# Fetching the first tokens ahead of the constants, on two queues, in chunks of 128

## The chip, the cores and the metric

The kernel runs on one core of one Trainium2 chip. The metric is the device time of one execution in microseconds (us); the times given are the median of three runs, and a profile is one further execution taken by the hardware profiler.

## What is computed

A decoder trunk of two layers over 1024 tokens, with 16 learned meta tokens put ahead of them (1040 rows of 1024 float32 values). Layer 0 mixes tokens with a gated DeltaNet, layer 1 with an mLSTM; each layer is then followed by a squared-ReLU MLP. Cut to what matters here, which is the very first step of layer 0:

```python
h = concatenate([meta, x], axis=1)              # (1, 1040, 1024)
y = h * rsqrt(mean(h * h, axis=-1) + 1e-6) * attn_norm[0]
proj = y @ gdn_in[0]                            # q, k, v, z, beta and a of 16 heads
qkv = silu(causal_conv(qkv, gdn_conv[0]))       # depthwise, 4 taps
# ... chunked delta rule, gated norm, output projection, residual, MLP; then layer 1
```

## The kernel before

Everything is float32, and large products are made in three passes: an operand is split into a high part in the rounded type float32r and a low part (what the rounding left), and `mm3` issues high times high, high times low and low times high (lines 116 to 118). Weights come in columns of 128: `load_split` fetches a column into a raw buffer (line 153), ACT casts the high part `whi` (line 156), and DVE subtracts for the low part `wlo` (line 157). There are two raw buffers and two pairs of split buffers.

The DeltaNet layer works on two halves of the tokens. The first half has 528 tokens (16 meta tokens and 512 of x), the second 512. For each half, `proj` runs through eight head pairs with several columns each. The first columns are K and Q of the first pair, and each takes all tokens of the half in two groups: `dense` makes eight times three products for a group, into the tile `ps_in`. Both groups of the first half have 264 tokens. The order at the very start is K group 0, Q group 0, K group 1, Q group 1, then the gate column (`gates_dense`, lines 138 and 139), then V.

Before any of that, the tokens must be normed, turned and split. `load_consts` builds masks on POOL and fetches the small norm and convolution vectors as rows (lines 208 to 212, on SP's queue); PE transposes them (line 215, tile `ps_nr`), and DVE copies them to `ncols` (line 217). Then `norm_in` takes the 528 tokens in five chunks: four of 112 and one of 80. For every chunk:

- SP's queue fetches the rows into a tile `nx` (lines 303 and 304);
- ACT squares them and sums (line 319), DVE scales the sum (line 320), POOL takes the power -1/2 (line 321), and DVE multiplies the rows by it (line 322);
- PE transposes the eight blocks of 128 columns into two PSUM tiles `pn` (line 329); the pool has two such tiles in all;
- for each of the two, DVE multiplies by the norm weights in `ncols` (line 331, tile `xw`), ACT casts the high part (line 334, tile `act_hi`) and DVE subtracts for the low part (line 335, tile `act_lo`).

The order of instructions on each engine is not the order of this text. A planner simulates the program with estimated times and writes each engine's instructions in the order that it finds; on the chip every engine then runs them strictly in that order, waiting on semaphores. Each DMA is issued by one engine's queue (here SP, and for a few transfers in the MLPs ACT).

Of the kernel before, what the change touches and what calls it, by code (L numbers as in the profile page):

```python
# [7 lines left out]
F32 = mybir.dt.float32  # L8
F32R = mybir.dt.float32r
AF = mybir.ActivationFunctionType  # L10
ALU = mybir.AluOpType
# [4 lines left out]
P = 128  # L16
D = 1024
KT = D // P
SEQ = 1024
META = 16  # L20
# [11 lines left out]
GS = 2 * GC  # L32
GL = (META + GC * P, GC * P)
GO = (META, 0)
XW = GL[0]
FF = 4096
HB = 4
# [18 lines left out]
class Ctx:  # L56
# [29 lines left out]
    def xact(self):  # L86

        return tuple(self.acts.tile([P, 2, XW], F32R, tag=t, name="act_" + t) for t in ("hi", "lo"))

# [93 lines left out]
def load_consts(c, attn_norm, ffn_norm, mlstm_norm, gdn_norm, gdn_conv):  # L183
    nc, k = c.nc, c.const
    c.ident = k.tile([P, P], F32, name="ident")
    make_identity(nc, c.ident)
    c.ones = k.tile([P, P], F32, name="ones")
    nc.gpsimd.memset(c.ones, 1.0)
    c.eps = k.tile([P, 1], F32, name="eps")
    nc.gpsimd.memset(c.eps, EPS)  # L190
    warm = k.tile([P, 1], F32, name="warm")
    nc.scalar.activation(warm, c.eps, AF.Square)
    c.rt = k.tile([NT, 2 * G // NT], F32, name="rt")
    c.half = k.tile([P, 1], F32, name="half")
    nc.gpsimd.memset(c.half, 0.5)
    c.mhalf = k.tile([P, 1], F32, name="mhalf")
    nc.gpsimd.memset(c.mhalf, -0.5)
    c.tri = k.tile([P, P], F32, name="tri")
    nc.gpsimd.memset(c.tri, 1.0)
    nc.gpsimd.affine_select(out=c.tri, in_=c.tri, pattern=[[1, P]], compare_op=ALU.is_ge, fill=0.0,  # L200
                            base=0, channel_multiplier=-1)
    c.mneg = k.tile([P, P], F32, name="mneg")
    nc.gpsimd.memset(c.mneg, 0.0)
    nc.gpsimd.affine_select(out=c.mneg, in_=c.mneg, pattern=[[1, P]], compare_op=ALU.is_ge, fill=NEG,
                            base=0, channel_multiplier=-1)
    rows = staging(c, [P, 2, P])
    nc.gpsimd.memset(rows[:, 1], 0.0)
    nc.sync.dma_start(out=rows[:, 0], in_=gdn_conv[0].rearrange("t (c p) -> (t c) p", p=P))
    nc.sync.dma_start(out=rows[0:16, 1], in_=attn_norm.rearrange("l (k p) -> (l k) p", p=P))
    nc.sync.dma_start(out=rows[16:32, 1], in_=ffn_norm.rearrange("l (k p) -> (l k) p", p=P))  # L210
    nc.sync.dma_start(out=rows[32:40, 1], in_=mlstm_norm.rearrange("l (k p) -> (l k) p", p=P))
    nc.sync.dma_start(out=rows[40:41, 1], in_=gdn_norm)
    ps = c.pj.tile([P, 2, P], F32, tag="pj", name="ps_nr")
    for j in range(2):
        nc.tensor.transpose(ps[:, j], rows[:, j], c.ident)
    cols = k.tile([P, 2, P], F32, name="ncols")
    nc.vector.tensor_copy(cols, ps)
    c.conv_w = cols[:, 0].rearrange("p (t c) -> p t c", t=4)
    c.attn_nw = [cols[:, 1, l * KT:(l + 1) * KT] for l in range(2)]
    c.ffn_nw = [cols[:, 1, 16 + l * KT:16 + (l + 1) * KT] for l in range(2)]  # L220
    c.mlstm_nw = cols[:, 1, 32:40]
    c.gdn_nnw = k.tile([P, 1], F32, name="gdn_nnw")
    nc.vector.tensor_scalar(c.gdn_nnw, cols[:, 1, 40:41], -1.0, None, op0=ALU.mult)


class GDN:
# [69 lines left out]
            nc.vector.tensor_copy(t, bc(self.idq, 1, GS))  # L296
            yield

    def x_rows(self, t0, n, xt=None):
        xt = (staging(self.c, [P, D]) if xt is None else xt)[:n]  # L300
        m = max(META - t0, 0)
        if m:
            self.nc.sync.dma_start(out=xt[0:m], in_=self.meta)
        self.nc.sync.dma_start(out=xt[m:n], in_=self.x[t0 + m - META:t0 + n - META])
        return xt

    def norm_in(self):

        nc, c, g2 = self.nc, self.c, self.g2
        self.xh = [c.xact() for _ in range(KT // 2)]  # L310
        tags = ("AB", "AB", "V", "V", "sz")
        rows = 112
        spans = [(t0, min(rows, GL[0] - t0)) for t0 in range(0, GL[0], rows)]
        junk = g2.tile([P, D], F32, tag="sz", name="njunk", bufs=3)
        xs = [self.x_rows(t0, n, g2.tile([P, D], F32, tag=tg, name="nx", bufs=3 if tg == "sz" else 2))
              for (t0, n), tg in zip(spans, tags)]
        for (t0, n), xt in zip(spans, xs):
            ss = self.p2.tile([P, 1], F32, tag="xs1", name="xs1", bufs=len(xs))[:n]
            nc.scalar.activation(junk[:n], xt, AF.Square, accum_out=ss)
            nc.vector.tensor_scalar(ss, ss, 1.0 / D, EPS, op0=ALU.mult, op1=ALU.add)  # L320
            nc.gpsimd.tensor_tensor(ss, ss, c.mhalf[:n], op=ALU.pow)
            nc.vector.tensor_scalar(xt, xt, ss[:, 0:1], None, op0=ALU.mult)
        for (t0, n), xn in zip(spans, xs):
            ts = slice(t0, t0 + n)
            for kk in range(2):
                ks = slice(kk * 4, kk * 4 + 4)
                pn = self.pp.tile([P, 4, P], F32, tag="pp", name="pn")[:, :, :n]
                for j in range(4):
                    nc.tensor.transpose(pn[:, j], xn[:, (kk * 4 + j) * P:(kk * 4 + j + 1) * P], c.ident[:n, :n])
                xw = self.p2.tile([P, 4, rows], F32, tag="raw", name="xw")[:, :, :n]  # L330
                nc.vector.tensor_tensor(xw, pn, bc(c.attn_nw[0][:, ks], 2, n), op=ALU.mult)
                for j in range(2):
                    hi, lo = (t[:, :, ts] for t in self.xh[2 * kk + j])
                    nc.scalar.copy(hi, xw[:, 2 * j:2 * j + 2])
                    nc.vector.tensor_tensor(lo, xw[:, 2 * j:2 * j + 2], hi.bitcast(F32), op=ALU.subtract)

    def h_init(self, cc):
# [3 lines left out]
        if cc >= HC:  # L341
            for kk in range(2):
                junk = self.p2.tile([P, XW], F32, tag="acc", name="xjunk")[:CH, :D // 2]
                nc.scalar.activation(junk, xt[:, kk * (D // 2):(kk + 1) * (D // 2)], AF.Square,
# [29 lines left out]
    def norm_pair(self, j):  # L374
# [4 lines left out]
        for i in range(2):  # L379
            k = 2 * j + i  # L380
            hk = self.p2.tile([P, 3 + XW], F32, tag="raw", name="hk")[:, :n]
            nc.sync.dma_start(out=hk, in_=self.dram["hT"][k, :, T - n:T])
# [6 lines left out]
    def gates_dense(self, hf):  # L389
# [6 lines left out]
        w = gates_split(c, wraw)  # L396
        self.ba = self.p1.tile([P, XW], F32, tag="ba", name="ba")
        for g in range(2):
# [4 lines left out]
    def tokens(self, hf, ci):  # L403

        t0 = GO[hf] + ci * P if ci < GC else 0
        return slice(t0, t0 + P)
# [56 lines left out]

    def dense(self, whl, hf, g):

        c, n = self.c, GL[hf] // 2
        ps = c.pj.tile([P, 512], F32, tag="pj", name="ps_in")[:, :n]
        gs = slice(g * n, (g + 1) * n)
        for k in range(KT):
            xhi, xlo = (x[:, k % 2, gs] for x in self.xh[k // 2])  # L470
            if isinstance(whl, tuple):
                mm3(self.nc, ps, whl[0][:, k], whl[1][:, k], xhi, xlo, k == 0, k == KT - 1)
            else:
                mm2(self.nc, ps, whl[:, k], xhi, xlo, k == 0, k == KT - 1)
            if k == KT // 2 - 1:
                yield
        return ps, gs

    def column(self, s, ct, out):
# [3 lines left out]
        n = GL[s["hf"]]  # L483
        raw = p2.tile([P, 3 + XW], F32, tag="raw", name="raw")
        nc.gpsimd.tensor_copy(raw[:, 0:3], self.hist[:, ct])
# [4 lines left out]
        if s["hf"] == 0:  # L490
            nc.gpsimd.tensor_copy(self.hist[:, ct], raw[:, n:n + 3])
        acc = p2.tile([P, XW], F32, tag="acc", name="acc")[:, :n]
        cw = c.conv_w[:, :, ct:ct + 1]
# [1192 lines left out]
def trunk(tc, x, meta_tokens, attn_norm, ffn_norm, ff_up, ff_down, gdn_in, gdn_conv, gdn_a_log, gdn_dt_bias,  # L1686
          gdn_norm, gdn_out, mlstm_in, mlstm_gate_bias, mlstm_norm, mlstm_out, out):
    nc = tc.nc
    with ExitStack() as st:
        c = Ctx(tc, st)  # L1690
        c.const = c.pool("const", 1)
        dp = c.pool("dram", 1, space=DRAM)
        dram = {
            "hT": dp.tile([KT, P, T], F32, name="d_hT"),
            "o": dp.tile([16, P, T], F32, name="d_o"),
            "cum": dp.tile([2, 16 * (GC + 1), P], F32, name="d_cum"),
            "rr": dp.tile([HC, CH], F32, name="d_rr"),
            "a": [[dp.tile([P, 2, 2, 2, g], F32, name=f"d_a{l}_{i}") for i in range(FF // P // 2)]
                  for l, (_, g) in enumerate((ALL, REAL))],
        }  # L1700
# [6 lines left out]
        ast = ExitStack()  # L1707
        c.acts = c.pool("acts", 5, ast)
        c.pj = c.pool("pj", 2, space=PSUM)
        load_consts(c, attn_norm, ffn_norm, mlstm_norm, gdn_norm, gdn_conv)  # L1710
        gdn = GDN(c, x[0], meta_tokens, gdn_in[0], gdn_a_log, gdn_dt_bias, gdn_out[0], dram)
        units, unit = gdn.run()
        xa, nst, dst = ExitStack(), ExitStack(), ExitStack()
        norm = Norm(c, c.pool("nrm", 1, nst, side="right"), c.ffn_nw[0])
# [14 lines left out]
        m = MLSTM(c, mlstm_in[0], mlstm_gate_bias, mlstm_out[0], after.norm.x, mdram)  # L1729
# [29 lines left out]
```

## Time and profile before

| what | value |
|---|---|
| time, median of 3 runs | 3062.37 us (3059.59 to 3062.48) |
| time of the profiled execution | 3060.66 us |
| its span in the profile | 3059.0 us |
| PE busy in the span | 2990.9 us (98%) |
| mean granted TensorE clock | 0.995 of full speed |

The span is the time from the first to the last instruction that the profiler saw; the profiled execution took 1.66 us more than its span, which lies outside the program. PE is TensorE's matmul row, DVE VectorE, ACT ScalarE, POOL GpSimd, SP the engine that issues most DMAs. Matmuls are pipelined, so one product's shown duration is longer than the distance to the next product's start; that distance is what a product costs.

### The profile page before, as it was taken

Reading aid. Unit: us, or ns where it says so; the run is one execution under the profiler, and the core shown is the slowest. Engines: PE = TensorE matmul, PEld = TensorE weight load, DVE = VectorE, ACT = ScalarE, POOL = GpSimd, SP = SyncE. Lnnn points to the kernel's source line nnn. Section 1 sums busy time; section 2 is a strip of 40 time slices with the busy share of each in tenths; the row PEclk is TensorE's granted clock in tenths of the full one; section 3 lists DMA queues with packets and bytes.
Section 4 is the critical chain, followed back from the end, with each engine's and each line's share of the span. In section 5 each row is a group of like instructions: output and inputs, shape, how many; then the busy total and the mean of one; then the engine's idle time right before and its main releaser. Section 6 shows DMA issues by size and latency. Waiting matters only on the chain. (4 is left out here: it accounts for less than half of the span.)

```text
span 3059.0 us, 63498 instructions
## 1 busy us (share of the span) xinstructions
PE 2990.9 (98%) x25790; PEld 2837.8 (93%) x25790; DVE 1931.9 (63%) x4395; ACT 1470.8 (48%) x3356; POOL 302.6 (10%) x534
## 2 busy tenths in 40 slices
PE   7999999999999998999999999999999899999999
PEld 7999998999999998999999999999998899978887
DVE  6866778777787568765644447333468876654443
ACT  5666767666665445654411114444445555521122
POOL 2323332222231000000000000000000000000000
PEclk9999999999999999999999999999999999999999
DMA  4332333233334733443422312222133344342223
GB/s 111 87 89 80 91 85 92 82 94 101 82 96 149 240 108 91 144 120 108 150 90 87 103 63 84 64 63 63 61 101 88 118 125 121 121 138 82 94 87 104
DMA packets 401892, 310.22 MB, mean 101 GB/s; under 512 B 29855, under 2 KB 366112, under 8 KB 401600
## 3 DMA queue, kind: packets, MB, share of 16 engines
q1 hardware_dynamic: 366000, 272.32, 30.3%
q10 hardware_dynamic: 35600, 33.84, 3.2%
q8 instruction: 204, 3.34, 0.5%
q14 instruction: 88, 0.72, 0.1%
HBM read 247.79 MB, written 58.31 MB: 100 GB/s over the span
## 5 line engine op out<-in xcount | busy, mean ns | idle before, releaser
L116 PE MATMUL ps_up<-xhi,uop 128*128 128x260 f32 (+1 forms) x1792 | 508.3, 285 | 20.7 <-DVE up_u L1106 6.9
L118 PE MATMUL ps_up<-xhi,uop 128*128 128x260 f32 (+1 forms) x1792 | 506.0, 283 | 5.1 <-DVE uop L1095 5.1
L117 PE MATMUL ps_up<-xlo,uop 128*128 128x260 f32 (+1 forms) x1792 | 507.0, 283 | 0.4 <-DVE xlo L1043 0.4
L116 PE MATMUL ps_dn<-act_hi,whi 128*128 128x260 f32 (+1 forms) x1536 | 493.5, 321 | 0.6 <-DVE up_c L1106 0.5
L156 ACT CAST whi<-wraw 128x1024 fp32r<-128x1024 f32 (+1 forms) x248 | 256.0, 1033 | 491.3 <-PE ps_dn L117 361.4
L117 PE MATMUL ps_dn<-act_lo,whi 128*128 128x260 f32 (+1 forms) x1536 | 491.4, 320 | 0.0
L118 PE MATMUL ps_dn<-act_hi,wlo 128*128 128x260 f32 (+1 forms) x1536 | 490.4, 319 | 0.0
L116 PE MATMUL ps_in<-act_hi,whi 128*128 128x264 f32 (+1 forms) x1536 | 452.0, 294 | 2.9 <-ACT raw L488 1.9
L118 PE MATMUL ps_in<-act_hi,wlo 128*128 128x264 f32 (+1 forms) x1536 | 447.7, 291 | 0.0
L117 PE MATMUL ps_in<-act_lo,whi 128*128 128x264 f32 (+1 forms) x1536 | 446.9, 291 | 0.0
L157 DVE TENSOR_TENSOR wlo<-wraw,whi 128x1024 fp32r<-128x1024 f32 (+1 forms) x248 | 300.7, 1213 | 169.3 <-ACT whi L156 163.9
L1203 DVE TENSOR_TENSOR hT<-hT,ps_dn 128x260 f32<-128x260 f32 (+1 forms) x384 | 195.1, 511 | 325.9 <-PE ps_dn L118 325.3
L116 PEld LDWEIGHTS ps_up<-xhi,uop 128*128 128x128 f32 x1792 | 339.7, 190 | 25.7 <-issue 7.4
L118 PEld LDWEIGHTS ps_up<-xhi,uop 128*128 128x128 f32 x1792 | 339.5, 190 | 6.2 <-DVE uop L1095 6.2
L117 PEld LDWEIGHTS ps_up<-xlo,uop 128*128 128x128 f32 x1792 | 340.2, 190 | 0.8 <-DVE xlo L1043 0.8
L118 PEld LDWEIGHTS ps_dn<-act_hi,wlo 128*128 128x128 f32 x1536 | 289.4, 188 | 24.3
L116 PEld LDWEIGHTS ps_dn<-act_hi,whi 128*128 128x128 f32 x1536 | 288.8, 188 | 23.3 <-DVE up_c L1106 0.7
L117 PEld LDWEIGHTS ps_dn<-act_lo,whi 128*128 128x128 f32 x1536 | 288.7, 188 | 22.3
L116 PEld LDWEIGHTS ps_in<-act_hi,whi 128*128 128x128 f32 x1536 | 290.8, 189 | 7.5 <-ACT raw L488 2.5
L117 PEld LDWEIGHTS ps_in<-act_lo,whi 128*128 128x128 f32 x1536 | 290.9, 189 | 2.8 <-issue 0.6
L118 PEld LDWEIGHTS ps_in<-act_hi,wlo 128*128 128x128 f32 x1536 | 290.7, 189 | 2.4 <-issue 0.4
L116 PE MATMUL ps_m<-act_hi,whi 128*128 128x260 f32 (+1 forms) x768 | 224.2, 292 | 0.8 <-ACT mso L1472 0.8
(398 smaller groups left out, 6396.8 us busy)
## 6 DMA issues: line engine op xcount, KB each, us to landing
wraw<-in_gdn_in_dram SPq DMA_DIRECT2D x96, 512.0 KB, 4.0
wraw<-in_ff_down_dram SPq DMA_DIRECT2D x72, 512.0 KB, 3.4
wraw<-in_ff_up_dram SPq DMA_DIRECT2D x42, 512.0 KB, 4.6
r<-in_ff_up_dram SPq DMA_DIRECT2D x42, 512.0 KB, 4.5
a_st<-d_a SPq DMA_DIRECT2D x32, 520.0 KB, 3.6
wraw<-in_gdn_out_dram SPq DMA_DIRECT2D x32, 512.0 KB, 4.2
a_st<-d_a SPq DMA_DIRECT2D x32, 512.0 KB, 5.4
wraw<-in_mlstm_in_dram SPq DMA_DIRECT2D x28, 512.0 KB, 3.8
```

The costliest lines, as they stand in the source:

```text
L116: nc.tensor.matmul(ps, whi, xhi, start=first, stop=False)
L117: nc.tensor.matmul(ps, whi, xlo, start=False, stop=False)
L118: nc.tensor.matmul(ps, wlo, xhi, start=False, stop=last)
L156: nc.scalar.copy(hi, raw)
L157: nc.vector.tensor_tensor(lo, raw, hi.bitcast(F32), op=ALU.subtract)
L1203: nc.vector.tensor_tensor(hT[:, d, t0:t0 + n], hT[:, d, t0:t0 + n], ps, op=ALU.add)
```

## The change

A new method `fetch_in` issues the fetches of the five token chunks; it is called before `load_consts`, and the chunks alternate between SP's and ACT's queue. The chunks become four of 128 tokens and one of 16. The five fetches of constants in `load_consts` move from SP's to ACT's queue. In `norm_in`, the multiplication of the rows stays on DVE for the first two chunks and goes to ACT for the other three, and five products of the identity with the second chunk's rows (128 x 512, plain float32), which nobody reads, are issued into a PSUM tile that is free at that time. The two groups of the first half become 256 and 272 tokens, so that group 0 is chunks 0 and 1 exactly; the second half keeps two groups of 256.

```diff
+GE = ((2 * P, GL[0]), (2 * P, GL[1]))
...
     rows = staging(c, [P, 2, P])
     nc.gpsimd.memset(rows[:, 1], 0.0)
-    nc.sync.dma_start(out=rows[:, 0], in_=gdn_conv[0].rearrange("t (c p) -> (t c) p", p=P))
+    nc.scalar.dma_start(out=rows[:, 0], in_=gdn_conv[0].rearrange("t (c p) -> (t c) p", p=P))
...
-    nc.sync.dma_start(out=rows[40:41, 1], in_=gdn_norm)
+    nc.scalar.dma_start(out=rows[40:41, 1], in_=gdn_norm)
...
-    def x_rows(self, t0, n, xt=None):
+    def x_rows(self, t0, n, xt=None, engine=None):
         xt = (staging(self.c, [P, D]) if xt is None else xt)[:n]
         m = max(META - t0, 0)
+        engine = engine or self.nc.sync
         if m:
-            self.nc.sync.dma_start(out=xt[0:m], in_=self.meta)
-        self.nc.sync.dma_start(out=xt[m:n], in_=self.x[t0 + m - META:t0 + n - META])
+            engine.dma_start(out=xt[0:m], in_=self.meta)
+        engine.dma_start(out=xt[m:n], in_=self.x[t0 + m - META:t0 + n - META])
         return xt
+
+    def fetch_in(self):
+
+        nc, g2 = self.nc, self.g2
+        tags = ("AB", "AB", "V", "V", "sz")
+        self.spans = [(t0, min(P, GL[0] - t0)) for t0 in range(0, GL[0], P)]
+        self.xs = [self.x_rows(t0, n, g2.tile([P, D], F32, tag=tg, name="nx", bufs=3 if tg == "sz" else 2),
+                               (nc.sync, nc.scalar)[i % 2])
+                   for i, ((t0, n), tg) in enumerate(zip(self.spans, tags))]
 
     def norm_in(self):
...
-        rows = 112
-        spans = [(t0, min(rows, GL[0] - t0)) for t0 in range(0, GL[0], rows)]
         junk = g2.tile([P, D], F32, tag="sz", name="njunk", bufs=3)
-        xs = [self.x_rows(t0, n, g2.tile([P, D], F32, tag=tg, name="nx", bufs=3 if tg == "sz" else 2))
-              for (t0, n), tg in zip(spans, tags)]
-        for (t0, n), xt in zip(spans, xs):
+        spans, xs, rows = self.spans, self.xs, P
+        for i, ((t0, n), xt) in enumerate(zip(spans, xs)):
             ss = self.p2.tile([P, 1], F32, tag="xs1", name="xs1", bufs=len(xs))[:n]
             nc.scalar.activation(junk[:n], xt, AF.Square, accum_out=ss)
             nc.vector.tensor_scalar(ss, ss, 1.0 / D, EPS, op0=ALU.mult, op1=ALU.add)
             nc.gpsimd.tensor_tensor(ss, ss, c.mhalf[:n], op=ALU.pow)
-            nc.vector.tensor_scalar(xt, xt, ss[:, 0:1], None, op0=ALU.mult)
+            if i < 2:
+                nc.vector.tensor_scalar(xt, xt, ss[:, 0:1], None, op0=ALU.mult)
+            else:
+                nc.scalar.activation(xt, xt, AF.Copy, scale=ss[:, 0:1])
+            if i == 1:
+
+                pw = self.mg.tile([P, 512], F32, tag="mg", name="warm")
+                for j in range(5):
+                    nc.tensor.matmul(pw, c.ident, xt[:, 0:512], start=True, stop=True)
...
     def dense(self, whl, hf, g):
 
-        c, n = self.c, GL[hf] // 2
-        ps = c.pj.tile([P, 512], F32, tag="pj", name="ps_in")[:, :n]
-        gs = slice(g * n, (g + 1) * n)
+        c = self.c
+        gs = slice(GE[hf][0] if g else 0, GE[hf][g])
+        ps = c.pj.tile([P, 512], F32, tag="pj", name="ps_in")[:, :gs.stop - gs.start]
...
+        gdn = GDN(c, x[0], meta_tokens, gdn_in[0], gdn_a_log, gdn_dt_bias, gdn_out[0], dram)
+        gdn.fetch_in()
         load_consts(c, attn_norm, ffn_norm, mlstm_norm, gdn_norm, gdn_conv)
-        gdn = GDN(c, x[0], meta_tokens, gdn_in[0], gdn_a_log, gdn_dt_bias, gdn_out[0], dram)
```

## Rows read from the trace of the kernel before

**Rows 1.** The page: busy time of the engines over the span.
```profile
PE 2990.9 (98%) x25790; PEld 2837.8 (93%) x25790; DVE 1931.9 (63%) x4395; ACT 1470.8 (48%) x3356; POOL 302.6 (10%) x534
```

**Rows 2.** Busy time by stretch: stretch, length, PE, PEld, DVE, ACT, POOL, clock, DMA share, GB/s.
```profile
0.00:20.00 20.00, 5.44 (x23) 3.87 (x23) 13.46 (x40) 11.05 (x22) 10.61 (x38) 1.00 0.64 166
20.00:40.00 20.00, 18.13 (x130) 17.79 (x131) 12.54 (x29) 7.37 (x21) 1.04 (x4) 1.00 0.27 59
40.00:60.00 20.00, 20.00 (x165) 19.89 (x164) 16.15 (x36) 12.77 (x20) 4.00 (x6) 1.00 0.36 94
```

**Rows 3.** Waits, 0 to 40 us: who waited for what, total, times, longest.
```profile
PE pn L329 <- DVE xw L331: 8.4, 4, 4.8
ACT njunk L319 <- DMA nx<-in_x_dram: 5.7, 4, 3.0
PE ps_nr L215 <- POOL hist L284: 2.9, 1, 2.9
PE ps_nr L215 <- DMA wraw<-in_gdn_conv_dram: 2.8, 1, 2.8
PE pn L329 <- DVE nx L322: 2.3, 1, 2.3
```

**Rows 4.** Timeline of PE, first large products: start, duration.
```profile
23.53 0.79 PE L116 MATMUL ps_in<-act_hi,whi 128*128 128x264 f32 x2
...
26.43 0.42 PE L118 MATMUL ps_in<-act_hi,wlo 128*128 128x264 f32 x1
...
26.65 0.42 PE L116 MATMUL ps_in<-act_hi,whi 128*128 128x264 f32 x1
...
38.22 0.28 PE L118 MATMUL ps_in<-act_hi,wlo 128*128 128x264 f32 x1
...
38.35 0.28 PE L138 MATMUL ps_in<-act_hi,wgate 128*128 128x264 f32 x1
```

**Rows 5.** Timeline of the first chunk, and the last low part.
```profile
5.34 1.06 ACT L319 ACTIVATE njunk<-nx 112x1024 f32<-112x1024 f32 x1 [3.04 <-DMA nx<-in_x_dram]
...
6.80 0.41 DVE L217 COPY ncols<-ps_nr 128x256 f32<-128x256 f32 x1
...
8.14 0.76 DVE L322 TENSOR_SCALAR nx<-nx,xs 112x1024 f32<-112x1024 f32 x1 [0.68 <-POOL xs L321]
...
8.95 1.75 PE L329 MATMUL pn<-ident,nx 112*128 112x112 f32 x8 [2.34 <-DVE nx L322]
...
11.10 1.15 DVE L331 TENSOR_TENSOR xw<-pn,ncols 128x448 f32<-128x448 f32 x2
...
29.75 1.03 DVE L335 TENSOR_TENSOR act_lo<-xw,act_hi 128x160 fp32r<-128x160 f32 x4
```

**Rows 6.** Busy time by stretch, as in 2, of DMA and DVE.
```profile
6.00:7.00 1.00, 0.45 (x1) 0.18 (x1) 1.00 (x10) 0.49 (x2) 0.32 (x2) 1.00 0.99 311
9.00:10.00 1.00, 1.00 (x6) 1.00 (x7) 0.15 (x1) 0.63 (x3) 0.26 (x1) 1.00 1.10 315
11.00:31.00 20.00, 11.92 (x69) 10.89 (x70) 16.23 (x40) 10.65 (x28) 4.53 (x6) 1.00 0.40 87
```

**Rows 7.** DMA issues, 0 to 40 us: count, KB each, us to landing.
```profile
nalog<-in_gdn_a_log_dram SPq DMA_DIRECT2D x1, 8.0 KB, 6.9
```

**Rows 8.** Groups by form, DVE, 10.9 to 31 us: count, busy, mean ns, idle before.
```profile
L322 DVE TENSOR_SCALAR nx<-nx,xs 112x1024 f32<-112x1024 f32 x3 | 2.3, 753 | 0.7 <-POOL xs L321 0.7
L331 DVE TENSOR_TENSOR xw<-pn,ncols 128x320 f32<-128x320 f32 x2 | 0.9, 492 | 1.5 <-PE pn L329 1.5
```

**Rows 9.** Timeline of SP's and ACT's issues.
```profile
3.78 1.79 SPq L304 DMA_DIRECT2D nx<-in_x_dram  x4
...
1303.95 0.38 ACTq L1113 DMA_DIRECT2D d_a<-up_c  x1
```

**Rows 10.** Timeline of PE around 1000 us.
```profile
1001.76 1.05 PE L791 MATMUL pst<-Yw,Kt 128*128 128x256 f32 x2
1002.61 1.06 PE L797 MATMUL po<-Y,AB 128*128 128x128 f32 x4
```

More of the change, by code (lines that the diff above doesn't have):

```diff
@@ L207, in load_consts @@
     nc.gpsimd.memset(rows[:, 1], 0.0)
-    nc.sync.dma_start(out=rows[:, 0], in_=gdn_conv[0].rearrange("t (c p) -> (t c) p", p=P))
-    nc.sync.dma_start(out=rows[0:16, 1], in_=attn_norm.rearrange("l (k p) -> (l k) p", p=P))
-    nc.sync.dma_start(out=rows[16:32, 1], in_=ffn_norm.rearrange("l (k p) -> (l k) p", p=P))
-    nc.sync.dma_start(out=rows[32:40, 1], in_=mlstm_norm.rearrange("l (k p) -> (l k) p", p=P))
-    nc.sync.dma_start(out=rows[40:41, 1], in_=gdn_norm)
+    nc.scalar.dma_start(out=rows[:, 0], in_=gdn_conv[0].rearrange("t (c p) -> (t c) p", p=P))
+    nc.scalar.dma_start(out=rows[0:16, 1], in_=attn_norm.rearrange("l (k p) -> (l k) p", p=P))
+    nc.scalar.dma_start(out=rows[16:32, 1], in_=ffn_norm.rearrange("l (k p) -> (l k) p", p=P))
+    nc.scalar.dma_start(out=rows[32:40, 1], in_=mlstm_norm.rearrange("l (k p) -> (l k) p", p=P))
+    nc.scalar.dma_start(out=rows[40:41, 1], in_=gdn_norm)
     ps = c.pj.tile([P, 2, P], F32, tag="pj", name="ps_nr")
@@ L310, in norm_in @@
         self.xh = [c.xact() for _ in range(KT // 2)]
-        tags = ("AB", "AB", "V", "V", "sz")
-        rows = 112
-        spans = [(t0, min(rows, GL[0] - t0)) for t0 in range(0, GL[0], rows)]
         junk = g2.tile([P, D], F32, tag="sz", name="njunk", bufs=3)
-        xs = [self.x_rows(t0, n, g2.tile([P, D], F32, tag=tg, name="nx", bufs=3 if tg == "sz" else 2))
-              for (t0, n), tg in zip(spans, tags)]
-        for (t0, n), xt in zip(spans, xs):
+        spans, xs, rows = self.spans, self.xs, P
+        for i, ((t0, n), xt) in enumerate(zip(spans, xs)):
             ss = self.p2.tile([P, 1], F32, tag="xs1", name="xs1", bufs=len(xs))[:n]
```

## The prediction

> **What bounds the kernel now.** I read the page first: PE is busy for 2990.9 of 3059.0 us [rows 1], so 68.1 us of the span are idle on the engine that sets the time. The busy times by stretch show where: 14.6 us of it lie in the first 20 us and 1.9 us in the next 20 (16.4 us in all), and from 40 us on PE is full, with 165 products in 20 us, 0.121 us each [rows 2]. The other 51.7 us are spread over the 3000 us behind. So the change can win what it takes from the first 40 us, and no other stage is touched.
>
> The waits say what PE waits for there: first the constants (2.8 and 2.9 us before the two transposes of `ps_nr`), then the first normed chunk (2.3 us), and most of all, 8.4 us in four waits, for DVE to free the two `pn` tiles [rows 3]. The timeline of PE gives the mark by which I count. The first large product starts at 23.53; 96 of them (K and Q, both groups) lie before the first gate product at 38.35 [rows 4]. At 0.121 us they would take 11.6 us, and they take 14.8: between 23.5 and about 27.8 they start 0.22 us apart (26.43 and 26.65 [rows 4]), which for 264 columns is the 1.2 GHz level though the clock column says 1.00, and transposes of the last two chunks lie between them. Everything behind the gate product is a full PE, so a gain at 38.35 is a gain at the end. I call this time the mark.
>
> DVE is what the mark hangs on. From its first `xw` at 11.10 to its last `act_lo` at 30.78 [rows 5] it is nearly full: 16.2 of 20 us [rows 6]. Ahead of that, the first chunk's chain runs from the square at 5.34 over the scaled rows (8.14) and eight transposes (8.95 to 10.70) to that `xw` [rows 5]; `ncols`, which `xw` needs as well, is there from 7.2 on [rows 5] and costs nothing now.
>
> **The change, part by part.**
>
> *The fetches.* SP issues a fetch in 0.45 us (1.79 for four [rows 9]); seven issues leave the head of its queue or go to ACT's, so chunk 0 is asked for about half a microsecond sooner, chunk 1 three sooner. ACT's nearest issue took 0.38 us [rows 9]; seven of them make 2.7 us, ACT's own idle time before its first square is 3.04 us [rows 5], and that square now waits for the landing, not for ACT. If that cover were gone, each issue would cost 0.38. But one queue alone already keeps the 16 DMA engines at 0.99 to 1.10 of their time, with 311 to 315 GB/s [rows 6], so a second adds no bytes. Both queues together must move 2.2 MB of tokens; at some 300 GB/s from about 2.0 us that is 7.2 us, to 9.2. Chunks 0 and 1 share the first half and land near 5.8: no better than the 5.34 of now for chunk 0, 2.5 us better for chunk 1.
>
> *The constants* are the price. They now stand on ACT's queue behind chunks 1 and 3, a megabyte. What that does to a small transfer the issues show: the 8 KB of `nalog`, put behind the chunks on SP's queue, took 6.9 us to land [rows 7]. So the constants land at about 9.5 us; two transposes and the copy (0.4 us each, with the hand-overs 1.4 in all [rows 5]) make `ncols` ready at 10.9. The wait for the first chunk goes, and the wait for `ncols` is late in its place: the first `xw` starts at 10.9 where it now starts at 11.10. The bounds: not before 10.3 (chunk 0's own chain, with its square at 5.8: 3.6 us to the transposes as now, 0.9 for the first four of them), and 12.7 if `ncols` stands ahead of the first sum in DVE's order, since then the scaling of chunk 0, its power and its first transposes (about 2 us) begin only when the constants are there.
>
> The Trainium skill says the same of the two queues in "DMA: Bandwidth & Descriptors", section "Issuing engines are not separate DMA queues": transfers from SP and ACT run on the same 16 engines and interleave, and issuing from both saves only the issuing time. That speaks against the change's main step, and the shares of 0.99 to 1.10 [rows 6] agree with it; were it wrong, the constants would land some 3 us sooner and the first rival below would hold.
>
> *Three multiplications* leave DVE: 0.753 us each [rows 8], 2.3 us off the engine that sets the mark. On ACT they cost about as much as the square, 1.06 us [rows 5], so 3.2 us; ACT was busy for 10.7 of the 20 us from 11 to 31 [rows 6], so they fit. If they stand ahead of casts that DVE waits for, up to 1.06 us comes back; with them in gaps, nothing does.
>
> *Chunks of 128 and 16.* As many tokens, as many instructions: the `xw`, `act_hi` and `act_lo` work per token stays. I cost it at nothing; the short last chunk saves a few tenths of fixed time at most.
>
> *Groups of 256 and 272.* Eight columns less in one product and eight more in the other, 0.0033 us each way at 2.4 GHz: nothing, over 1168 pairs. What the split gives is that K group 0 no longer waits for a third chunk.
>
> *The five unused products.* The nearest row is two plain float32 products of 256 columns in 0.85 us [rows 10], so one of 512 takes 0.85 and five 4.3 us. They become ready with chunk 1's rows, at about 9.8, and fill time in which PE now idles (up to 4.8 us at a time [rows 3]). They can hold up chunk 1's transposes until about 14, some 1 to 1.5 us late, which DVE can bridge with the low part of K's weights. What they can give is the 2.4 GHz level for the first large products: 19 of them 0.1 us faster, 1.9 us. That counts only if PE, not DVE, sets the mark.
>
> **The sum.** DVE's work behind the first `xw` is now 16.1 us, with 3.6 us of gaps. Take off the three multiplications: 13.8. I keep gaps of 3.4 us, because the order is planned from estimates again, with the wait for the last chunk's transposes (1.5 us [rows 8]) still in it. So the last `act_lo` ends at 10.9 + 13.8 + 3.4 = 28.1, against 30.78. K group 1 needs all of tokens 256 to 527, hence all chunks, and can start about 0.4 us ahead of that end; 48 products follow, 5.8 us. The mark comes at 33.5 instead of 38.35, **4.8 us sooner**.
>
> Does PE keep up? K group 0 can start at about 18.0 (chunks 0 and 1 are half of DVE's token work, plus the first weights), its 48 products and Q's end 5.8 us later, with 20 transposes among them (0.11 us each once fast) at about 26.0, and at 27.9 if slow: before 28.1. So DVE sets the mark, and the unused products are worth nothing in this sum. The profiled execution of 3060.66 us (span 3059.0) becomes 3055.9; its time was 1.7 below the median of the runs, and from the median of 3062.4 the forecast is **3057.6 us**, 0.16% faster. A measurement of this kernel can tell about 0.2% (6.1 us) from no change, so the likeliest outcome falls inside that.
>
> **The rivals.**
>
> *A: PE sets the mark and the whole cover works.* If DVE's gaps shrink to 1 us and the first `xw` starts at 10.3, its work ends at 25.1; then PE decides, with K group 0 from 17.5, 5.8 us for group 0, 2.2 of transposes and 5.8 for group 1, at 31.3: 7.0 us, 3055.4. For it: the multiplications and the sums behind which DVE waited 0.7 us and more [rows 8] move off its path; the constants are a few small rows. Against it: DVE's gaps in the present order, and the 6.9 us of `nalog` [rows 7].
>
> *B: the gain is eaten in the start.* `ncols` ahead of the first sum in DVE's strict order (2 us) and chunk 1's transposes behind the unused products (1.5 us) put the mark at 37.0: 1.3 us, 3061. For it: today `ncols` does stand ahead of the scaling of chunk 0 (6.80 and 8.14 [rows 5]). Against it: the planner sees the constants' fetches issued last. This is also the case in which the change does not do what it says: the tokens come first and are not used first.
>
> *C: slower.* The planner writes the order of all later steps anew, from start times that have moved. PE idles for 51.7 us behind the first 40 [rows 1, 2]; if the new order makes that a fifth more, 10.9 us, the start's gain is gone and 6.1 us more with it, 3068.5. It decides from 10.9 us on; up to 4.8 it only eats the gain. For it: no order outside the start is pinned. Against it: the work of the later steps and their buffers are the same, and PE is full there.
>
> **Chances.** The forecast (a gain of 2.5 to 6.1 us) 0.45, A 0.36, B with other small losses 0.12, C 0.07. Faster by over 0.2% is A, 0.36; within 0.2% are the forecast and B, 0.57; slower is C, 0.07. The forecast's own range is 3056.3 to 3059.9. For 8 in 10 I go down past A by the fast clock's 1.9 us, to 3053.2, and up past B by half of what the runs differ (2.9 us from lowest to highest), to 3062.5.
>
> **What the profile should show.** The first square at 5.5 to 6.3, the first two squares back to back; `ncols` at 10 to 12, after the scaled rows of chunk 0 (before them in B); the first `xw` near 11; five products of `warm` between 9 and 15; the first large product at 17 to 19; the last `act_lo` at 27 to 29 (25 in A); the first gate product at 33 to 35; behind it PE full, and the same idle time from 40 us on. I am wrong if the constants land well before chunk 3, if ACT rather than DVE is full from 11 to 28, or if idle time behind 40 us differs by more than 3 us.

## The result, and the profile after

The changed kernel takes 3080.51 us (median of 6 runs, 3073.84 to 3084.52); the kernel before takes 3062.24 beside it (6 runs, 3059.59 to 3063.2). The ratio is 1.0054, with an interval of 1.0044 to 1.0065: slower by 18 us, where 3057.6 was forecast. The profiled execution took 3080.5 us, its span 3078.8 against 3059.0.

The page of the changed kernel: span, and busy time of the engines.

```profile
span 3078.8 us, 63523 instructions
...
PE 3003.3 (98%) x25800; PEld 2844.5 (92%) x25800; DVE 1930.2 (63%) x4392; ACT 1474.1 (48%) x3359; POOL 303.9 (10%) x534
```

The instruction counts stand nearly as in [rows 1]: ten products more on PE, three multiplications fewer on DVE and three more on ACT. PE is busy for 12.4 us more, of which the unused products make about 6, and idle for 7.4 us more (75.5 against 68.1). The busy times by stretch, with columns as in [rows 2]:

```profile
0.00:20.00 20.00, 6.89 (x18) 4.10 (x19) 9.26 (x31) 10.72 (x19) 8.73 (x38) 1.00 0.62 171
20.00:40.00 20.00, 17.40 (x140) 16.20 (x139) 14.07 (x34) 9.77 (x25) 0.79 (x3) 1.00 0.16 42
40.00:60.00 20.00, 20.00 (x167) 19.89 (x166) 15.34 (x33) 12.83 (x22) 3.17 (x6) 1.00 0.35 97
```

Against [rows 2], DVE has 4.2 us less work in the first 20 us. The three multiplications that went to ACT are 2.3 us of it (all five stood there before); the rest is a late start. The timeline of the start tells why (start, duration, engine, line; ACTq is ACT's queue of issues; in brackets the idle time before and what ended it):

```profile
1.25 0.93 ACTq L307 DMA_DIRECT2D nx<-in_x_dram  x2
...
3.07 0.32 ACTq L212 DMA_DIRECT2D wraw<-in_ffn_norm_dram  x1
...
7.40 0.51 ACTq L213 DMA_DIRECT2D wraw<-in_mlstm_norm_dram  x1
...
10.45 0.23 ACTq L214 DMA_DIRECT2D wraw<-in_gdn_norm_dram  x1
10.73 1.06 ACT L327 ACTIVATE njunk<-nx 128x1024 f32<-128x1024 f32 x1 [7.02 <-DMA nalog<-in_gdn_a_log_dram]
...
13.55 1.97 PE L345 MATMUL pn<-ident,nx 128*128 128x128 f32 x8 [9.75 <-DVE xs L328]
...
15.23 1.22 DVE L159 TENSOR_TENSOR wlo<-wraw,whi 128x1024 fp32r<-128x1024 f32 x1 [0.17 <-ACT whi L158]
...
15.31 0.42 PE L217 MATMUL ps_nr<-ident,wraw 128*128 128x128 f32 x1
...
15.53 5.89 PE L338 MATMUL warm<-nx,ident 128*128 128x512 f32 x10
...
16.37 0.42 DVE L219 COPY ncols<-ps_nr 128x256 f32<-128x256 f32 x1
...
16.90 1.28 DVE L347 TENSOR_TENSOR xw<-pn,ncols 128x512 f32<-128x512 f32 x2
```

ACT's five small fetches of constants are not issued one behind the other. The fourth goes out at 7.40 and the fifth at 10.45, and ACT's first square, with ACT idle for 7.02 us, stands behind them. The first chunk's chain begins 5.4 us later than in [rows 5], and the first `xw` comes at 16.90 (11.10 before). The name in the bracket, `nalog`, is that of the last event before the square; ACT was held by its own queue, as 10.45 and 10.73 show.

PE then, two of its first large products (the first of all starts at 23.91) and the first gate product (the mark):

```profile
25.02 0.28 PE L119 MATMUL ps_in<-act_lo,whi 128*128 128x256 f32 x1
25.14 0.28 PE L120 MATMUL ps_in<-act_hi,wlo 128*128 128x256 f32 x1
...
39.14 0.28 PE L140 MATMUL ps_in<-act_hi,wgate 128*128 128x256 f32 x1
```

From 24.79 on they start 0.12 us apart, the 2.4 GHz level, where [rows 4] show 0.22. The mark comes 0.8 us later than in [rows 4]. So the start accounts for 0.8 of 19.8 us, and 19 us are lost behind it.

To place them, I matched products by tile and count (the n-th product into `ps_out` in one trace against the n-th in the other) and took the difference of their starts. `ps_in` 2304 lies 32 products ahead of the first one of the second half of the tokens (458 us before), `ps_out` 0 the output projection of the DeltaNet layer (919 us), `ps_m` 0 the mLSTM (1874 us). Differences to the kernel before, in us, one profiled execution each; the kernels other than the changed one are those of the experiments:

| kernel | mark | ps_in 2304 | ps_out 0 | ps_out 768 | ps_m 0 | span |
|---|---|---|---|---|---|---|
| the change | +0.8 | +6.4 | +13.9 | +16.0 | +17.2 | +19.8 |
| split alone (groups) | -0.4 | +3.1 | +11.8 | +15.5 | +18.6 | +21.2 |
| change without split (start_only) | +1.2 | +1.5 | +1.4 | +1.5 | +1.4 | +2.0 |
| split, order of before (split_old_order) | +0.1 | -0.6 | -0.8 | -0.2 | -1.0 | +2.2 |
| before, order of the split (old_split_order) | -0.3 | +7.3 | +12.3 | +15.7 | +16.2 | +17.5 |
| the change, order of before (after_old_order) | +0.3 | -0.4 | +0.1 | +3.4 | +3.1 | +6.5 |
| split in K and Q of the first pair (g256_kq) | -0.8 | -0.5 | -0.6 | 0.0 | -1.6 | +1.1 |
| groups of 260 and 268 (g260) | +0.3 | +8.3 | +14.0 | +12.6 | +12.5 | +16.3 |
| gate copies on DVE (n1) | -0.5 | +1.3 | +7.7 | +11.5 | +11.7 | +11.2 |
| repaired start (repaired) | +0.1 | +0.6 | +0.8 | +2.4 | -0.2 | -0.6 |
| start_only, no unused products (start_nowarm) | +2.8 | +4.6 | +5.1 | +5.0 | +4.7 | +6.3 |
| repaired, split in first K and Q (best) | -3.7 | -2.1 | -1.7 | +1.3 | -0.8 | +1.1 |
| the same, order of before (best_old_order) | -3.1 | -1.4 | -1.0 | +2.7 | +1.1 | +5.1 |

Single executions of one kernel differ by some 3 us either way, so the last columns of a row are no finer than that; the times below are medians. Within the layer, where another order puts other work before the n-th product, the difference also swings from one product to the next: for the change it is +1.3 us at `ps_in` 2200, +6.4 at 2304 and +8.0 at 2336, the first product of the second half. The DeltaNet layer takes 13 of the 19 us. About half of that, 6 to 7.5 us, is lost in its second half, where both kernels use groups of 256. That cannot be the shape of those products; it has to be what stands around them. The order did change: of DVE's some 4150 instructions about 3470 stand in the same sequence in both traces (the longest sequence common to both), and nine in ten of the others lie between 100 and 1062 us, in the DeltaNet layer and the output projection that ends it.

### The profile page after: what moved, and what is told of

It reads as the page before. It is cut to its first block, busy times and chain, and to the rows that moved or that the text cites. A ratio compares the mean times of both kernels' runs of the same rounds, so it can differ in the third digit from the quotient of the medians.

```text
span 3078.8 us, 63523 instructions
## 1 busy us (share of the span) xinstructions
PE 3003.3 (98%) x25800; PEld 2844.5 (92%) x25800; DVE 1930.2 (63%) x4392; ACT 1474.1 (48%) x3359; POOL 303.9 (10%) x534
## 5 line engine op out<-in xcount | busy, mean ns | idle before, releaser
L118 PE MATMUL ps_in<-act_hi,whi 128*128 128x256 f32 (+1 forms) x1536 | 452.7, 295 | 5.5 <-ACT raw L504 2.7
L119 PE MATMUL ps_in<-act_lo,whi 128*128 128x256 f32 (+1 forms) x1536 | 447.1, 291 | 0.0
L120 PE MATMUL ps_in<-act_hi,wlo 128*128 128x256 f32 (+1 forms) x1536 | 446.6, 291 | 0.0
L118 PEld LDWEIGHTS ps_in<-act_hi,whi 128*128 128x128 f32 x1536 | 291.3, 190 | 11.7 <-ACT sz L565 4.5
```

The costliest lines, as they stand in the source:

```text
L118: nc.tensor.matmul(ps, whi, xhi, start=first, stop=False)
L119: nc.tensor.matmul(ps, whi, xlo, start=False, stop=False)
L120: nc.tensor.matmul(ps, wlo, xhi, start=False, stop=last)
```

## Which part costs: the split or the start

**Theory O (order).** The split changes the planner's estimated times of all products of the first half, it writes another order for the whole layer, and that order is worse. **Rival S (sizes).** Products of 256 and 272 columns, or what reads them, cost more by themselves. **Rival T (start).** The late start costs, and the rest follows from it.

*The split alone.*

```diff
 GO = (META, 0)
+GE = ((2 * P, GL[0]), (2 * P, GL[1]))
...
-        ps = c.pj.tile([P, 512], F32, tag="pj", name="ps_in")[:, :n]
-        gs = slice(g * n, (g + 1) * n)
+        gs = slice(GE[hf][0] if g else 0, GE[hf][g])
+        ps = c.pj.tile([P, 512], F32, tag="pj", name="ps_in")[:, :gs.stop - gs.start]
```

> The kernel before with the groups of 256 and 272 alone; fetches, chunks and multiplications as before. Order theory (the split makes the planner write another order for the whole DeltaNet layer, and that order costs there): first gate product near 38.4 us as before, then 10 to 15 us lost up to the output projection, 3073 to 3082 us in all. Start theory (the late start costs the layer, the split nothing): 3059 to 3065 us.

Measured: 3081.94 us (3080.33 to 3083.66), ratio 1.006 [1.0048, 1.0073]. The mark is 0.4 us sooner, and the whole loss is there.

*The change without the split.*

```diff
-GE = ((2 * P, GL[0]), (2 * P, GL[1]))
+GE = ((GL[0] // 2, GL[0]), (2 * P, GL[1]))
```

> The change without the split: both groups keep 264 tokens; fetches on two queues, chunks of 128, constants on ACT's queue, unused products all as changed. Order theory: the layer runs in the order of before, so only the start counts; first square near 10.7 as in the changed kernel, first gate product at 38.5 to 40, 3060 to 3066 us. Start theory: as slow as the changed kernel, 3077 to 3084 us.

Measured: 3064.61 us, ratio 1.0008 [0.9999, 1.0016]. The distance stays at 1.2 to 1.5 us from the mark to the mLSTM: a delay at the start is carried along as it is. T is out as the cause of the loss; it is the split.

## Sizes or order

The decisive runs exchange the two. In the first, the kernel has the split, and every instruction is tied to the one that stands before it on its engine in the other kernel's order, so that the planner has nothing left to choose. In the second, the kernel before gets the split's order in the same way. The programs then hold the same instructions, engine by engine, in the same places. In short:

```diff
         trunk(tc, *args, out)
+        pin(tc, nc)
...
+def pin(tc, nc):
+    at = {i.name: i for i in nc.cur_bb.bb.instructions}
+    for engine in orders:                   # names in the wanted order, one list for each engine
+        for prev, name in zip(engine, engine[1:]):
+            tc.add_manual_dep(at[name], prev, mybir.DependencyInfo(
+                mybir.DependencyClass.NoSync, mybir.DependencyReason.DATA), reason="order")
```

> The split alone (256 and 272), with every engine's instructions held in the order of the kernel before, instruction for instruction; nothing else differs. If the order is what costs (theory O), the loss of the split alone goes: the mark at 37.6 to 38.4, the distance to before constant from there, 3061 to 3065 us (ratio 0.999 to 1.001). If the sizes themselves cost (theory S: products of 256 and 272 columns run worse than two of 264), it stays near 3080 (ratio 1.005 and more), with about 12 us of it in the DeltaNet layer.

> The kernel before, two groups of 264, with every engine's instructions held in the order that the split alone got. Theory O: the loss comes without the split, 3076 to 3084 us (ratio 1.004 to 1.007), most of it between 39 us and ps_out 0 and more behind. Theory S: about 3063 (ratio 0.999 to 1.001).

Measured: the split in the order of before takes 3062.38 us (3058.52 to 3066.8), ratio 0.9995 [0.9986, 1.0004]. Two groups of 264 in the order of the split take 3082.78 (3073.97 to 3084.51), ratio 1.0058 [1.0045, 1.0071]. The loss goes with the order and leaves with it. S is out: the 256 and 272 columns are worth nothing that can be measured, either way. The orders of all engines were exchanged together, so which engine's order costs is not shown.

The layer's stretch (40 us to `ps_out` 0) shows it in one row for each kernel; columns as in [rows 2]. The kernel before, then the changed kernel:

```profile
40.00:919.00 879.00, 871.22 (x9525) 818.83 (x9524) 661.99 (x2056) 586.46 (x1679) 256.31 (x442) 1.00 0.32 90
```

```profile
40.00:933.00 893.00, 878.99 (x9535) 824.04 (x9534) 664.96 (x2069) 588.50 (x1684) 259.05 (x443) 0.99 0.32 89
```

The split in the order of before, then the sizes of before in the split's order:

```profile
40.00:918.00 878.00, 870.07 (x9524) 817.61 (x9523) 662.11 (x2056) 586.95 (x1679) 258.02 (x442) 1.00 0.32 90
```

```profile
40.00:931.00 891.00, 877.31 (x9523) 822.43 (x9522) 664.07 (x2067) 586.78 (x1681) 259.19 (x443) 1.00 0.32 88
```

PE's idle time is 7.8 and 7.9 us in the order of before (879 less 871.22, 878 less 870.07), and 14.0 and 13.7 us in the split's order. The other 7 to 8 us of the loss stand as busy time, in the exchanged pair for the same products (the changed kernel's stretch has ten more, some 1.2 us). In the changed kernel the granted clock explains a part. By stretches of 10 us through the layer, before has one below 0.97 (0.83 from 120 to 130), the changed kernel four:

```profile
130.00:140.00 10.00, 8.43 (x115) 8.11 (x113) 6.89 (x27) 8.46 (x18) 4.51 (x9) 0.83 0.20 55
...
220.00:230.00 10.00, 9.21 (x62) 8.86 (x61) 6.40 (x34) 8.85 (x20) 1.73 (x4) 0.84 0.34 91
...
580.00:590.00 10.00, 9.34 (x77) 7.73 (x76) 7.32 (x24) 7.93 (x15) 4.54 (x10) 0.92 0.35 117
590.00:600.00 10.00, 10.00 (x73) 9.45 (x72) 7.47 (x34) 6.19 (x19) 0.69 (x1) 0.91 0.23 60
```

A mean of 0.83 is a third of the stretch at 1.2 GHz. Three of the four have idle time of PE in them. Summed over the layer, one less the clock makes 1.7 us before and 5.1 us after. So of 14 us, 6 are idle, some 3.4 the clock and 1.2 the ten products; the remaining 3 or so lie in products that start further apart, which neither column shows. The clock is no fixed part of what the order costs: the same sum is 3.4 us for the sizes of before in the split's order and 1.7 us, as before, for the split alone, and both lose as much. Of the 6 us of idle time, the waits of PE in that stretch of the changed kernel (who waited for what, us, times, longest) say this:

```profile
PE pot L754 <- ACT o L746: 2.6, 2, 1.7
PE ps_in L118 <- ACT sz L565: 2.5, 4, 0.8
PE pks L791 <- DVE S L810: 2.0, 2, 1.5
PE py L761 <- DVE R L796: 1.7, 3, 1.0
PE x L685 <- ACT Gm L679: 1.6, 1, 1.6
```

They are many small waits for ACT or DVE, none over 1.7 us, and most of them in the delta rule. No one of them is the cause; why this order has more of them than the other was not taken apart further.

*The whole change, in the order of before* from behind the start (DVE's first 60 instructions are left to the planner):

> The whole change, with the order behind the start (from the first 60 DVE instructions on) held as in the kernel before. Theory O: only the start's 0.8 us at the mark is lost, 3062 to 3066 us (ratio 1.000 to 1.001). Theory S: near 3080 (ratio 1.005).

Measured: 3065.61 us (3062.23 to 3068.05), ratio 1.0008 [0.9999, 1.0017], against 1.0054 for the change itself. The change's whole measurable loss is the order. In the one trace the distance is constant up to `ps_out` 0 (+0.1); 3.3 us then go in the output projection, to which the next section comes back.

**How far does an order depend on small things?** Three runs answer. One splits only K and Q of the first pair, where it matters for the start (the lines that matter, against the split alone; the comment is not in the program):

```diff
-        gs = slice(GE[hf][0] if g else 0, GE[hf][g])
+        e = GE[hf] if first else (GL[hf] // 2, GL[hf])     # first: K and Q of pair 0, first half
+        gs = slice(e[0] if g else 0, e[g])
```

> The kernel before with groups of 256 and 272 only in the K and Q columns of the first pair, 264 in all others. By its instruction lists this keeps the order of before almost everywhere. Order theory: 3058 to 3064 us. If unequal groups cost by their mere presence in the first columns, 3066 us or more.

Measured: 3061.5 us, ratio 0.9993 [0.9984, 1.0002]. 4154 of DVE's 4157 instructions keep their sequence, and nothing is lost. One splits at 260, which is a smaller change of size (against the split alone):

```diff
-GE = ((2 * P, GL[0]), (2 * P, GL[1]))
+GE = ((260, GL[0]), (2 * P, GL[1]))
```

> The kernel before with groups of 260 and 268. Size theory: half the imbalance, so nothing to half of the split's 19 us, 3062 to 3073 us, and the loss only in the first half of the layer (tokens of the first half). Order theory: another order again, so any shift from -5 to +25 us, and part of it in the second half, whose groups are 256 and 256 in all kernels.

Measured: 3077.09 us (3074.08 to 3079.89), ratio 1.0041 [1.0027, 1.0055]. And one leaves all sizes as they were and moves four small copies of the gate column from ACT to DVE:

```diff
-            nc.scalar.copy(self.ba[:, gs], ps)
+            nc.vector.tensor_copy(self.ba[:, gs], ps)
```

> The kernel before, groups of 264 kept; the only edit is that four small copies (the gate column out of PSUM, two per half) go to DVE instead of ACT. The work is the same, but by its instruction lists the planner's order differs from before from the second pair on (3528 of 4157 DVE instructions in the same sequence, against 2877 with the split). Order theory: the first 100 us as before, then a shift of several us in either direction across the DeltaNet layer, 3055 to 3080 us. Size theory (products of 256 and 272 themselves cost more than two of 264): 3060 to 3065 us, no shift in the layer.

Measured: 3070.61 us (3068.68 to 3073.12), ratio 1.0023 [1.0014, 1.0033]. Counted in the traces as above, about 3780 DVE instructions keep their sequence (the 3528 of the expectation is too low), and only one that does not lies before 460 us; the distance is +1.3 us at `ps_in` 2304 and +7.7 at the end of the layer. The copies themselves cannot be the loss: one takes 0.42 us on DVE against 0.38 on ACT. Each of the three other orders that ran is worse than that of before, by 0.23 to 0.6%. The order of before is a good one; that every other is worse is not shown by three.

## What the start is worth

*Constants first, on ACT; all tokens on SP; groups of 264.* No constant then stands behind a chunk, and nothing holds ACT.

```diff
-        gdn.fetch_in()
         load_consts(c, attn_norm, ffn_norm, mlstm_norm, gdn_norm, gdn_conv)
+        gdn.fetch_in()
...
-                               (nc.sync, nc.scalar)[i % 2])
+                               nc.sync)
```

> The start without the hold, groups of 264: the constants are issued first, on ACT's queue, all token chunks on SP's, chunks of 128, three multiplications on ACT and the unused products as changed. If ACT was held by the issues of the constants, its first square starts at 5 to 6 us, ncols is there by 8, the first xw starts at 9 to 10.5, the first gate product at 32 to 35, and the time is 3054 to 3059 us. If instead the tokens' landing held it, the square stays near 10 and the time at 3060 or more.

Measured: 3064.98 us (3058.83 to 3066.82), ratio 1.0002 [0.9993, 1.0011]. The first square starts at 5.10 instead of 10.73, so the issues did hold ACT. But `ncols` is copied only at 12.40, since it stands in DVE's order behind the sum of the fourth chunk, which waits for ACT. With groups of 264 the first large product has to wait for the third chunk as well; it comes at 24.15 and the mark at 38.50, 0.15 us later than in [rows 4] and not at the 32 to 35 expected.

*The unused products*, taken out of the change without the split:

```diff
-                pw = self.mg.tile([P, 512], F32, tag="mg", name="warm")
-                for j in range(5):
-                    nc.tensor.matmul(pw, c.ident, xt[:, 0:512], start=True, stop=True)
```

> start_only without the five unused products (groups of 264). If they hold up chunk 1's transposes, those start near 17.5 instead of 20.0, the second pair of xw near 19 instead of 22.3, and the first gate product comes 1 to 3 us sooner than the 39.6 of start_only, less up to 2 us for the first products at the lower clock level; the time 3060 to 3064 us. If they only fill a wait, the transposes stay at 20 and the gate product comes later, at 40 to 42.

Measured: 3066.45 us, ratio 1.0006 [0.9997, 1.0015], where it is 1.0008 with them: no difference in the times. In the traces there is one. The timeline of PE without them, the second chunk's transposes and large products:

```profile
17.69 1.94 PE L340 MATMUL pn<-ident,nx 128*128 128x128 f32 x8 [1.97 <-DVE xw L342]
...
27.79 0.42 PE L118 MATMUL ps_in<-act_hi,whi 128*128 128x264 f32 x1
28.01 0.42 PE L119 MATMUL ps_in<-act_lo,whi 128*128 128x264 f32 x1
```

and with them:

```profile
20.00 1.04 PE L345 MATMUL pn<-ident,nx 128*128 128x128 f32 x8
...
27.29 0.29 PE L118 MATMUL ps_in<-act_hi,whi 128*128 128x264 f32 x1
27.41 0.28 PE L119 MATMUL ps_in<-act_lo,whi 128*128 128x264 f32 x1
```

They hold up the transposes by 2.3 us and bring products 0.12 us apart instead of 0.22. The mark is 39.59 with them and 41.11 without: 1.5 us to the good in these two executions, where 1 to 3 us sooner without them was expected.

*The repaired start with the split in K and Q of the first pair*, which keeps the order nearly as it was:

> repaired, with the groups of 256 and 272 only in the K and Q columns of the first pair, which keeps the order of before in the DeltaNet layer. The first large product then waits for chunks 0 and 1 only: 20 to 22 us instead of 24.15, the first gate product at 35.5 to 37.5 instead of 38.5, the shift constant across the layer, and 3056 to 3062 us. If DVE's last low part (30.5 in repaired) sets the gate product anyway, it stays at 37.5 or more.

Measured: 3062.15 us (3059.65 to 3071.14), ratio 0.9999 [0.999, 1.0008]. Its timeline has what the change was forecast to have:

```profile
5.68 1.06 ACT L327 ACTIVATE njunk<-nx 128x1024 f32<-128x1024 f32 x1 [2.93 <-DMA nx<-in_x_dram]
...
11.21 0.42 DVE L219 COPY ncols<-ps_nr 128x256 f32<-128x256 f32 x1
...
11.74 1.28 DVE L347 TENSOR_TENSOR xw<-pn,ncols 128x512 f32<-128x512 f32 x2
...
18.72 0.50 PE L118 MATMUL ps_in<-act_hi,whi 128*128 128x256 f32 x2
```

The mark is at 34.67, 3.7 us sooner, and it stays so up to 373 us. Then 1.6 us go by `ps_in` 2304, and 3.0 us in the output projection. Is that the order again? The same kernel, with the order of before held from behind the start:

> The repaired start (constants first on ACT, all tokens on SP, the split only for K and Q of the first pair), with the order behind the start held as in the kernel before. If its 3.7 us at the mark were given back by the order (theory O), they now last: the distance to before stays at -3.5 to -3.9 to the end, 3058 to 3060.5 us (ratio 0.9985 to 0.9992). If they are given back by something else, as the waits for weights, which do not come sooner when PE does (theory W), the distance shrinks again in the same places, 3061 to 3063 (ratio 0.9995 to 1.0002).

Measured: 3063.7 us (3055.33 to 3069.11, 11 runs), ratio 1.0001 [0.9991, 1.0011]. The distance shrinks in the same two places. But the run says little more than `best` did: in the traces the two stand in one order, the same on DVE, ACT, POOL and both queues and for 25797 of PE's 25800 products. `best` had the order of before already (4143 of its 4152 DVE instructions keep their sequence), and that is what rules theory O out here.

*The first place is the granted clock.* The kernel before, `best`, and the one with the order held, from 370 to 390 us:

```profile
370.00:380.00 10.00, 10.00 (x107) 8.48 (x97) 6.49 (x21) 6.30 (x20) 2.46 (x5) 1.00 0.26 83
380.00:390.00 10.00, 10.00 (x86) 9.17 (x84) 6.34 (x24) 7.72 (x23) 8.42 (x15) 1.00 0.21 69
```

```profile
370.00:380.00 10.00, 10.00 (x83) 8.17 (x82) 8.29 (x26) 4.74 (x14) 5.03 (x9) 0.94 0.50 151
380.00:390.00 10.00, 10.00 (x71) 9.46 (x70) 6.21 (x27) 7.82 (x18) 5.06 (x9) 0.89 0.00 0
```

```profile
370.00:380.00 10.00, 10.00 (x86) 8.06 (x85) 7.76 (x25) 5.24 (x17) 4.38 (x8) 0.97 0.46 147
380.00:390.00 10.00, 10.00 (x68) 9.44 (x68) 6.43 (x27) 7.29 (x17) 5.68 (x10) 0.86 0.02 4
```

PE is full in all three and waits for nothing, so theory W does not cover it either. One less the clock makes 1.7 us in each of the last two and nothing in the first: the 1.6 us that go. The kernel with the gate copies on DVE has the same there, 0.83 from 380 to 390, and goes from -0.3 to +1.3. Why the clock falls there in some programs and not in others is not shown.

*The second place stays open.* In the output projection PE's waits from 975 to 1045 us show where. The kernel before, then the one with the order held:

```profile
PE ps_out L116 <- ACT act_hi L883: 1.4, 1, 1.4
PE ps_out L116 <- DVE hx L925: 0.9, 1, 0.9
```

```profile
PE ps_out L118 <- ACT act_hi L900: 4.3, 2, 3.5
PE ps_out L118 <- DVE hx L942: 1.4, 1, 1.4
```

That cast `act_hi` works on a tile, `ost`, that is fetched back from memory, and the DMA engines are full in this stretch (a share of 1.00 from 1020 to 1040, 0.98 before). SP's queue stands 5.7 us there for earlier fetches of `ost` to land, 2.6 us before. That would fit theory W, a gain that ends at the next stretch that fetches bound. But the whole change in the order of before comes to this stretch at +0.1 us, with no gain to lose, and loses 3.3 us in it with the same waits (3.9 us for `act_hi`, 5.4 us of SP's queue for `ost`). So being early is not what it takes, and W is not shown. The split in the order of before passes the place with a loss of 0.6 us. This kernel's 11 times spread over 13.8 us.

## Why the prediction was wrong

**The step that failed** is the cost of the groups of 256 and 272: "nothing, over 1168 pairs". For the products themselves that was right (0.9995 in the order of before). What it left out is that these lengths are what the planner orders by. Rival C had the mechanism, with the chance of 0.07, and put it down to moved start times. Its argument against, "the work of the later steps and their buffers are the same, and PE is full there", is what the runs refute. With the same work and the same buffers, the order alone costs 19 us (3082.78 against 3063.46). C's price was the point from which it decides, 10.9 us of idle time. Idle time grew by only 7.4 in all, and the rest is in clock and spacing. Moved start times were not what did it: with the start changed and the sizes kept (start_only), the distance stayed constant. The premise beside it, that a gain at the mark is a gain at the end, was not borne out either: the repaired start that is 3.7 us sooner there measured 0.9999 [0.999, 1.0008].

**The fetches: a second failed step.** "That square now waits for the landing, not for ACT" took ACT's issues as 0.38 us each. In the program the later of the small fetches carry a wait for the completion counter of an earlier transfer, out of eight counters used in turn. The fourth on ACT's queue waits for the counter of chunk 1, the fifth for that of chunk 3, and ACT, which runs strictly in order, stands behind its own issue. SP's fetch of `nalog` waits in the same way for chunk 0, and went out at 7.16. So chunk 0 had landed by then (5.8 was forecast, 5.1 and 5.7 are the first squares with all tokens on SP), and the square stood for another 3.5 us, to 10.73. The constants, landed by 9.5 in the sum, were not all issued before 10.45; and they did not only land late: they held the square, and through it all that follows. The first `xw` came at 16.90 instead of 10.9, a miss of 6.0 us. By the sum's own 4.5 us from the square to the first `xw` the square alone makes it 15.2. The other 1.7 us are `ncols`: its second transpose stood behind chunk 0's eight on PE (15.31), and its copy behind the first `wlo` on DVE (16.37). With the constants issued first, the first `xw` came at 11.74 and 12.93.

**The bytes** were nearly right. The fourth chunk lands at about 10.4 with two queues (the fifth issue waits for it), and with all tokens on SP at 9.8 and 11.0 (the ends of ACT's waits for it in the two repaired kernels): two queues bring no more, and they bring the first chunk later. The Trainium skill's rule in "DMA: Bandwidth & Descriptors", section "Issuing engines are not separate DMA queues", that issuing from two engines saves only the issuing time, agrees with that. The issue that holds up its engine cost more here. What the sum had too low is the rate, some 300 GB/s: at a full DMA share (1.01 to 1.04 from 6 to 8 us) 393 GB/s came with the two queues and 397 and 395 with one, all in chunks of 128 rows, against 303 before and 285 with the split alone, both in chunks of 112.

**DVE's sum** held. From the first `xw` to the last `act_lo` it took 16.1 us (16.90 to 33.0), forecast 17.2; DVE was busy for 12.9 of them, forecast 13.8. The three multiplications on ACT took 1.13 to 1.15 us each against 1.06. So 10.9 was the only term of the start that was off by much: 16.90 plus 16.1 plus the 6.1 to the mark is 39.14.

**The unused products** were mis-sized: 5.9 us, not 4.3. They ran at both levels, 0.86 us a record at first and 0.43 after, and each of the five is two records. The row behind the 0.85 us [rows 10] was misread: line 791 is one product of 256 columns in two records, not two products, and the granted clock from 1001 to 1003 us is 0.50. That 0.85 us is also the price of 512 columns at the upper level (two of 0.43) is luck. The sum held them worth nothing; 1.5 us at the mark is what they bring, near the 1.9 that the prediction gave as the most.

**Of B's two parts** one came about: chunk 1's transposes stood behind the unused products (21.26). `ncols` was not ahead of the first sum; it came behind the scaling of two chunks, in DVE's order behind sums that wait for ACT and behind `wlo`.

**Seen as foretold:** squares back to back, 0.12 us between the first large products, PE full behind the mark. "The same idle time from 40 us on" was the observation that decides, and it failed.

## What to carry to other kernels

Where a planner writes the order from estimated lengths, a change of a product's size can redraw the order of all that comes after; compare the instruction orders of the two programs before costing such an edit at nothing, and limit it to the few places where it is needed, or hold the old order. To separate sizes from order, run each size in the other's order, and follow matched products through the trace: here a delay at the start was a constant distance (start_only) and another order a growing one. Sum the granted clock of both traces before giving such a distance a cause: one stretch at the lower level is worth 1.7 us here. An issue on a compute engine's queue costs more than its issuing time when it has to wait for an earlier, larger transfer; put small fetches ahead of large ones (the square then started at 5.10 and 5.68), or, as the kernel before has it, on a queue that does not compute.

## What the runs showed of the hardware

- A DMA issue can hold its engine's computing for microseconds: ACT idled from 3.7 to 10.7 us behind issues of 4 KB and 0.5 KB, the last 3.5 us of it with its input in place.
- A plain float32 product of 512 columns is recorded as two, 0.86 us each at the 1.2 GHz level and 0.43 at 2.4 GHz.
- With PE full, the granted clock fell to a mean of 0.94 and 0.89 in two stretches of 10 us in one kernel (best, 370 to 390 us) and stayed at 1.00 in the kernel before; the products came 1.6 us later for it.
- The same instructions on every engine, in another order, differ by 0.6% here with PE's busy share at 97 and 98%: of 13 us in the layer, 6 are idle time, and the rest stands in the trace as busy.
